# Merging the four score stages of an HGRN2 unit into two runs on TensorE

## The chip, the cores and the metric

The kernel runs on one core of a Trainium2 chip. The metric is the device time of one execution in microseconds (us). Engines are named as in the profile: PE is TensorE (PEld its weight load), DVE is VectorE, ACT is ScalarE, POOL is GpSimd, and SP issues the DMA. Each engine works through its own instructions in the order in which they were built into the program; an instruction that has to wait holds everything behind it on its engine.

## The reference, cut to what matters

One mixer layer on a sequence of 2048 positions and 1024 features. One projection feeds three causal branches; their outputs, each times a SiLU gate, are joined, multiplied by `W_out`, added to the scaled input and normalised.

```python
h = jnp.einsum('bsd,de->bse', x, w_in)
a_u, a_v, a_g, b_val, b_glu, b_g, c_q, c_f, c_i, c_g = jnp.split(h, offsets, axis=-1)
y_a = _sgu_mixer(a_u, a_v, ...) * silu(a_g)          # A: gated 128x128 causal mixing
y_b = _conv_module(b_val, b_glu, ...) * silu(b_g)    # B: GLU, 31-tap causal convolution, LayerNorm
y_c = _hgrn2_mixer(c_q, c_f, c_i, lb, norm_g) * silu(c_g)
y = concat([y_a, y_b, y_c]) @ w_out
return layernorm(ALPHA * x + y)
```

The change is in branch C, a gated linear recurrence with 4 heads of width 128:

```python
f = lb + (1 - lb) * sigmoid(f_logit);  k = 1 - f;  q = silu(q)
# S_t = diag(f_t) S_{t-1} + k_t i_t^T ;  o_t = S_t^T q_t, in chunks:
scores[t, s] = sum_d q[t, d] * k[s, d] * prod(f[s+1 .. t, d])   for s <= t
o = scores @ i + (q * prod f) @ state
```

## The kernel before, in words

**Stages.** The sequence is worked in two halves of 1024 positions, each of two groups of G = 512. A half goes through branch B, branch A (first half here, second half at the end), the values of C (`values`) and then the 8 units of C, one for each head and group: 16 units in all, from about 205 us to 395 us and from about 505 us to 690 us of the span. The last stage is the output product, from about 757 us.

**Projections.** `proj_f` (lines 205 to 213) makes one 128x512 result from 24 matmuls (8 slices of the contraction, each as three products of split high and low parts) in one of 3 PSUM banks with the tag `mm`. A unit of C has three: `pm_f`, `pm_q` and `pm_cg`, 72 matmuls of 512 columns.

**What sets the order.** Around the projections the small steps of the units are woven in by a clock in the program that generates the kernel: after each slice of a projection `tick` moves it on by 0.64, so that a unit lasts 15.36 on it; `later(d, fn)` puts a step on a heap that is due d after now, and `tick` emits what is due (lines 178 to 194). The constants `DST0`, `DST`, `DKT`, `DPST`, `DPO` and `DPT` (line 47) are these delays for branch C. The framework's scheduler then orders each engine's instructions by its own costs; the matmuls marked `pinned` stay in the order in which they were emitted.

**A unit** (`hgrn_unit`, lines 358 to 586). `f` and `K` = 1 - f come from `pm_f` (a sigmoid on ACT, two multiplies on DVE). The silu of `pm_q` goes into the tile `X1`. The scores within a chunk are made by a tree of four stages with blocks of 1, 4, 16 and 64 positions. `stage(0)` and `stage(1)` are each a run of 16 matmuls with 32-column weights (line 406; 80 and 48 columns stream), `stage(2)` 8 with 64-column weights (line 441, 96 columns), `chunk_halves` 4 (line 501, 64 columns). All are fp32, which the profile counts as two instructions a matmul. Behind each run DVE copies the result out of its PSUM bank (tag `sc`, two banks) with `copy_predicated` into `S32` or `ST`, and raises `X`, `T` (products of f) and `K` to the next block size: `K` is multiplied in place, so that the next stage's matmuls read what the last one's DVE work has left. The next stage is due 5.5 later.

Then come `transposes` (`pk`, line 516, of K, in the one bank `tr`; ACT copies it out to `KT`), `states` (`pst`, line 532, in the one bank `st`; DVE makes the new states), `outputs` (`po`, lines 552 and 556, in the one bank `o`; ACT squares and scales it to `os`) and `finish` (`pt`, line 574, again in the one bank `tr`: transposes of `os`; DVE's L576 multiplies `pt` by the gate `sg` and reads the bank for that; then the result goes to DRAM). The bank `tr` is thus taken in turn by `pt` of one unit, `pk` of the next, and by `bb` of branch B's normalisation.

**The last stage's tiles.** `y_steps` loads the branches' outputs (`ry`), makes sums of them (`ysa`, `ysb`) in the pool `stiles`, and splits them into high and low parts; `free_c` closes the pools of C and loads the weights `wob` of the last stage into a new pool `w1`.

Of the kernel before, what the change touches and what calls it, by code (L numbers as in the profile page):

```python
# [11 lines left out]
F32 = mybir.dt.float32  # L12
# [8 lines left out]
P = 128  # L21
# [25 lines left out]
DST0, DST, DKT, DPST, DPO, DPT = 4.5, 5.5, 2.5, 2.0, 2.5, 6.0  # L47
# [37 lines left out]
def _body(tc, nc, d, ctx):  # L85
# [272 lines left out]
    def hgrn_unit(h, g, gi, w, x, pl, vh, ST, S32):  # L358
        nm = f"{h}_{g}"
        wf_, wq, wg = w  # L360
        pf = proj_f(wf_, x, f"f{nm}")
        f = pl.tile([P, G], F32, tag="f", bufs=2, name=f"f{nm}")
        nc.scalar.activation(f, pf, AF.Sigmoid)
        K = pl.tile([P, G], F32, tag="K", bufs=2, name=f"K{nm}")
        nc.vector.tensor_scalar(f, f, oml[:, h : h + 1], lb[:, h : h + 1], ALU.mult, ALU.add)
        nc.vector.tensor_scalar(K, f, -1.0, 1.0, ALU.mult, ALU.add)

        pq = proj_f(wq, x, f"q{nm}")
        X1 = pl.tile([P, P, 11], F32, tag="X1", bufs=1, name=f"X1{nm}")
        nc.scalar.activation(X1[:, :, 7:11], pq.rearrange("p (n j) -> p n j", j=4), AF.Silu)  # L370
        f3 = f.rearrange("p (n j) -> p n j", j=4)
        nc.vector.tensor_mul(X1[:, :, 0:2], X1[:, :, 7:9], f3[:, :, 0:2])
        nc.vector.tensor_mul(X1[:, :, 4:7:2], X1[:, :, 9:11], f3[:, :, 2:4])

        cur = {"X": X1.rearrange("p n (s b) -> p n s b", b=1), "T": f3}

# [15 lines left out]
        def stage(st):  # L392
            b = 4 ** st
            n = G // (4 * b)
            nsc = 10 if st == 0 else 6
            X, T = cur["X"], cur["T"]
            pc = bank("sc", 2, f"sc{nm}_{st}")
            if st < 2:
                npar = 32 // (4 * b)
                w_ = nsc * b * npar  # L400
                pcv = pc[:, : 4 * w_].rearrange("p (c w) -> p c w", c=4)
                for c in range(4):
                    for r in range(4):
                        lo_ = c * P + 32 * r
                        p0 = lo_ // (4 * b)
                        pinned(nc.tensor.matmul(pcv[32 * r : 32 * r + 32, c, :], K[:, lo_ : lo_ + 32],
                                         X[:, p0 : p0 + npar, 1 : 1 + nsc, :],
                                         start=True, stop=True))
# [22 lines left out]
                if st == 1:  # L431
                    for r in range(4):
                        rr = slice(32 * r, 32 * r + 32)
                        nc.scalar.copy(ST[rr, :, rr], S32[rr])
            else:
                w_ = nsc * b
                pcv = pc[:, : 4 * w_].rearrange("p (c w) -> p c w", c=4)
                for c in range(4):
                    for m in range(2):
                        lo_ = c * P + 64 * m  # L440
                        pinned(nc.tensor.matmul(pcv[64 * m : 64 * m + 64, c, :], K[:, lo_ : lo_ + 64],  # L441
                                         X[:, lo_ // 64, 1:7, :], start=True, stop=True))
                for i, (j0, s0, nj) in enumerate(((1, 0, 3), (2, 3, 2), (3, 5, 1))):
                    mo, mw = MOFF[6 + i]
                    for m in range(2):
                        rr = slice(64 * m, 64 * m + 64)
                        nc.vector.copy_predicated(  # L447
                            ST[rr, :, 64 * m + j0 * b : 64 * m + (j0 + nj) * b],
                            msk[rr, mo : mo + mw].unsqueeze(1).to_broadcast([64, 4, mw]),
                            pcv[rr, :, s0 * b : (s0 + nj) * b])  # L450

            if st < 2:
                nb = 4 * b
                Xn = pl.tile([P, n // 4, 7, nb], F32, tag=f"X{nb}", bufs=1, name=f"X{nb}_{nm}")
                Xj = X.rearrange("p (m k) s b -> p m k s b", k=4)
                Tj = T.rearrange("p (m k) j -> p m k j", k=4)
                for k0, sl in ((0, slice(0, 2)), (2, slice(4, 7, 2))):
                    nc.vector.tensor_copy(Xn[:, :, sl, 0:b], Xj[:, :, k0 : k0 + 2, 0, :])
                    nc.vector.tensor_mul(
                        Xn[:, :, sl, b : 4 * b],  # L460
                        Xj[:, :, k0 : k0 + 2, 1:4, :].rearrange("p m k s b -> p m k (s b)"),
                        Tj[:, :, k0 : k0 + 2, 0:1].to_broadcast([P, n // 4, 2, 3 * b]))
# [7 lines left out]
            nc.vector.tensor_mul(T[:, :, 2], T[:, :, 2], T[:, :, 3])  # L470
            nc.vector.tensor_mul(T[:, :, 1], T[:, :, 1], T[:, :, 2])
            Tn = pl.tile([P, n], F32, tag=f"T{4 * b}", bufs=2, name=f"T{4 * b}_{nm}")
            nc.vector.tensor_mul(Tn, T[:, :, 0], T[:, :, 1])
            K4 = K.rearrange("p (n j b) -> p n j b", j=4, b=b)
            if b == 1:
                nc.vector.tensor_mul(K4[:, :, 0:3, 0], K4[:, :, 0:3, 0], T[:, :, 1:4])
            else:
                nc.vector.tensor_mul(K4[:, :, 0:3, :], K4[:, :, 0:3, :],
                                     T[:, :, 1:4].unsqueeze(3).to_broadcast([P, n, 3, b]))
# [572 lines left out]
```

## Time and profile before

| | |
|---|---|
| time, median of 3 runs | 922.21 us (921.29 to 924.45) |
| the profiled execution: its time / its span | 923.13 us / 921.4 us |
| PE busy | 902.0 us, 98% of the span |
| DVE busy | 714.3 us, 78% |
| ACT busy | 392.6 us, 43% |
| granted PE clock, mean | 0.995 |

The span runs from the first to the last instruction; about 1.7 us of the execution lie around it. Busy time of PE counts a matmul from its start to its modelled end, and the ends overlap with the next start. So the start-to-start distances of the timeline tell what a matmul costs on PE, and idle time shows only where PE stood for longer than one matmul's tail.

### The profile page before, as it was taken

Reading aid. Unit: us, or ns where it says so; the run is one execution under the profiler, and the core shown is the slowest. Engines: PE = TensorE matmul, PEld = TensorE weight load, DVE = VectorE, ACT = ScalarE, POOL = GpSimd, SP = SyncE. Lnnn points to the kernel's source line nnn. Section 1 sums busy time; section 2 is a strip of 40 time slices with the busy share of each in tenths; the row PEclk is TensorE's granted clock in tenths of the full one; section 3 lists DMA queues with packets and bytes.
Section 4 is the critical chain, followed back from the end, with each engine's and each line's share of the span. In section 5 each row is a group of like instructions: output and inputs, shape, how many; then the busy total and the mean of one; then the engine's idle time right before and its main releaser. Section 6 shows DMA issues by size and latency. Waiting matters only on the chain.

```text
span 921.4 us, 15037 instructions
## 1 busy us (share of the span) xinstructions
PE 902.0 (98%) x5673; PEld 735.7 (80%) x5673; DVE 714.3 (78%) x1614; ACT 392.6 (43%) x774; POOL 81.9 (9%) x127
## 2 busy tenths in 40 slices
PE   8999999999999999999999999999999999999995
PEld 5889886887777877788888777877899887888885
DVE  6998898946787669997999867778785245898777
ACT  6524355143445336643314444443553343443450
POOL 0001200100010000001000000001012000221122
PEclk9999999999999999999999999999999999999998
DMA  8506797031112103521202111111151598555322
GB/s 267 179 26 222 256 313 235 35 115 36 36 46 70 35 13 127 162 68 58 69 1 92 46 47 47 47 46 47 47 173 58 189 333 277 166 181 181 135 92 91
DMA packets 60808, 107.43 MB, mean 117 GB/s; under 512 B 5312, under 2 KB 21952, under 8 KB 60608
## 3 DMA queue, kind: packets, MB, share of 16 engines
q1 hardware_dynamic: 60736, 106.48, 34.7%
q8 instruction: 44, 0.72, 0.3%
q14 instruction: 28, 0.23, 0.1%
HBM read 75.00 MB, written 31.46 MB: 116 GB/s over the span
## 4 chain that ended last, share of the span: by engine, by line
PE 74%; DVE 12%; DMA 5%; issue 3%; ACT 2%; POOL 2%; SPq 0%; POOLq 0%; DVEq 0%; ACTq 0%
DVE acc L285 5%; PE pm_q L201 3%; PE pm_ci L202 3%; PE pm_ci L203 3%; PE pm_ci L201 3%; PE pm_q L203 3%; PE pm_q L202 3%; PE pm_f L201 3%; PE poz L201 3%; PE pm_cg L201 3%; PE poz L203 3%; PE poz L202 3%; PE pm_f L203 3%; PE pm_cg L202 3%; PE pm_cg L203 3%
## 5 line engine op out<-in xcount | busy, mean ns | idle before, releaser
L285 DVE SCALAR_TENSOR_TENSOR acc<-bh,vec,acc 128x512 f32<-128x512 f32 x240 | 172.0, 748 | 2.7
L148 DVE TENSOR_TENSOR wl<-rw,wh 128x512 fp32r<-128x512 f32 x84 | 56.9, 687 | 19.1 <-ACT wh L147 18.9
L147 ACT CAST wh<-rw 128x512 fp32r<-128x512 f32 x84 | 50.1, 619 | 40.4 <-PE pm_f L202 11.1
L201 PE MATMUL pm_f<-xhix,wh 128*128 128x512 f32 x96 | 41.2, 429 | 0.0
L201 PE MATMUL pm_q<-xhix,wh 128*128 128x512 f32 x96 | 40.6, 423 | 0.0
L561 ACT ACTIVATE jk<-po 128x128 f32<-128x128 f32 x64 | 17.8, 277 | 51.6 <-PE po L556 50.6
L201 PE MATMUL pm_cg<-xhix,wh 128*128 128x512 f32 x96 | 38.9, 406 | 0.0
L203 PE MATMUL pm_f<-xhix,wl 128*128 128x512 f32 x96 | 37.7, 393 | 0.0
L202 PE MATMUL pm_q<-xlox,wh 128*128 128x512 f32 x96 | 37.7, 393 | 0.0
L202 PE MATMUL pm_f<-xlox,wh 128*128 128x512 f32 x96 | 37.6, 392 | 0.0
L203 PE MATMUL pm_q<-xhix,wl 128*128 128x512 f32 x96 | 37.6, 392 | 0.0
L201 PE MATMUL pm_ci<-wh_ci,xhix 128*128 128x512 f32 x96 | 37.6, 391 | 0.0
L203 PE MATMUL pm_cg<-xhix,wl 128*128 128x512 f32 x96 | 37.5, 391 | 0.0
L202 PE MATMUL pm_cg<-xlox,wh 128*128 128x512 f32 x96 | 37.5, 391 | 0.0
L203 PE MATMUL pm_ci<-wh_ci,xlox 128*128 128x512 f32 x96 | 37.4, 390 | 0.0
L202 PE MATMUL pm_ci<-wl_ci,xhix 128*128 128x512 f32 x96 | 37.4, 389 | 0.0
L227 POOL TENSOR_SCALAR crs<-ss 128x4 f32<-128x4 f32 x16 | 3.5, 217 | 362.1 <-ACT jk L561 362.1
L356 ACT COPY vh<-pm_ci 128x512 f32<-128x512 f32 x16 | 9.4, 589 | 56.6 <-PE pm_ci L203 56.6
L447 DVE COPY_PREDICATED ST<-msk,sc 64x192 f32<-64x192 int32 (+2 forms) x96 | 28.7, 299 | 5.3 <-PE sc L441 3.1
L504 ACT COPY ST<-sc 64x128 f32<-64x128 f32 x32 | 8.4, 261 | 50.9 <-PE sc L501 50.7
L566 ACT ACTIVATE os<-po,crs 128x128 f32<-128x128 f32 x64 | 18.3, 369 | 25.0 <-POOL crs L228 25.0
L201 PE MATMUL pm_av<-wh_av,xhix 128*128 128x256 f32 x96 | 28.2, 293 | 0.0
(355 smaller groups left out, 2745.6 us busy)
## 6 DMA issues: line engine op xcount, KB each, us to landing
rw<-wf SPq DMA_DIRECT2D x84, 256.0 KB, 3.2
wob<-wo_dr SPq DMA_DIRECT2D x14, 1024.0 KB, 11.3
xr<-x SPq DMA_DIRECT2D x16, 512.0 KB, 3.9
ry<-y_dr SPq DMA_DIRECT2D x32, 256.0 KB, 2.9
out<-xr SPq DMA_DIRECT2D x15, 512.0 KB, 2.6
wo_dr<-wsh SPq DMA_DIRECT2D x28, 256.0 KB, 3.2
wo_dr<-wsl SPq DMA_DIRECT2D x28, 256.0 KB, 3.0
rx<-xT SPq DMA_DIRECT2D x24, 256.0 KB, 3.4
```

The source lines that it names most:

```text
L147: nc.scalar.copy(hi, src)
L148: nc.vector.tensor_sub(lo, src, hi.bitcast(F32))
L201: nc.tensor.matmul(out, wh, xh, start=first, stop=False, **kw)
L202: nc.tensor.matmul(out, wh, xl, start=False, stop=False, **kw)
L203: nc.tensor.matmul(out, wl, xh, start=False, stop=last, **kw)
L227: nc.gpsimd.tensor_scalar(r, mv_var, scale, EPS, ALU.mult, ALU.add)
L285: nc.vector.scalar_tensor_tensor(a, h[:, k : k + G], vcol(cw + k), a, ALU.mult, ALU.add)
L356: nc.scalar.copy(vh[:, gi * 4 + tt, :], pt)
L447: nc.vector.copy_predicated(ST[rr, :, 64 * m + j0 * b : 64 * m + (j0 + nj) * b], msk[rr, mo : mo + mw].unsqueeze(1).to_broadcast([64, 4, mw]),
L504: nc.scalar.copy(ST[0:64, e:4:2, 64:128], pcv[64 * e : 64 * e + 64])
L561: nc.scalar.activation(jk, po[:, c * P : (c + 1) * P], AF.Square, accum_out=ss[:, c : c + 1])
L566: nc.scalar.mul(os_[:, c * P : (c + 1) * P], po[:, c * P : (c + 1) * P], rs[:, c : c + 1])
```

## The change

The four stages of the scores are cut into two runs. `near` is one run of 32 matmuls (stages of block 1 and 4) into one bank, `far` one of 12 (blocks of 16 and 64) into another. For that, what the second stage of a run needs is made ahead of it:

- a second copy of the keys, `L`, is written from `K` for block 4 as soon as f is there (one multiply of 256 elements and one of 128 a partition on DVE, one copy on ACT), where K was multiplied in place after the first stage by one multiply of 384. `L` is one buffer for all units.
- `raise_x` and `raise_t` are the former ends of the stages. `raise_x(0)` and `prep(1)` now stand ahead of the first run; `raise_x(1)`, `raise_t(1)`, `prep(2)`, `raise_x(2)` and `raise_t(2)` behind it.
- ACT's copies of a run (`side`: K's last quarter from `L`, and four copies of `S32` to `ST`) are emitted 4.5 behind the first run.
- the delays: the first run is due 7.0 after its X (before 4.5), the second 8.0 behind the first, the transposes 5.5 behind the second (2.5), the states 3.0 (2.0), the outputs 3.5 (2.5) and the finish 7.5 (6.0). From X to the finish of a unit it is 34.5 in all, before 34.0.
- `Q64` has two buffers in place of one, and the pool of the last stage's sums (`stiles`) is no longer a pool of its own but `w1`.

The diff, cut to its core (the three `copy_predicated` loops are as before):

```diff
-DST0, DST, DKT, DPST, DPO, DPT = 4.5, 5.5, 2.5, 2.0, 2.5, 6.0
+DNEAR, DFAR, DSIDE, DKT, DPST, DPO, DPT = 7.0, 8.0, 4.5, 5.5, 3.0, 3.5, 7.5
...
+        def raise_x(st):
...
+                for k0, sl in ((0, slice(0, 2)), (2, slice(4, 7, 2))):
+                    nc.vector.tensor_copy(Xn[:, :, sl, 0:b], Xj[:, :, k0 : k0 + 2, 0, :])
+                    nc.vector.tensor_mul(
...
+        def raise_t(st):
...
+            nc.vector.tensor_mul(d2, T[:, :, 2], T[:, :, 3])
+            nc.vector.tensor_mul(d1, T[:, :, 1], d2)
...
+            nc.vector.tensor_mul(Tn, T[:, :, 0], d1)
...
+        cur["T", 0] = f3
+        D = raise_t(0)
+        L = pl.tile([P, G], F32, tag="L", bufs=1, name=f"L{nm}")
+        K0 = K.rearrange("p (n j) -> p n j", j=4)
+        L0 = L.rearrange("p (n j) -> p n j", j=4)
+        nc.scalar.copy(L0[:, :, 3], K0[:, :, 3])
+        nc.vector.tensor_mul(L0[:, :, 0:2], K0[:, :, 0:2], D)
+        nc.vector.tensor_mul(L0[:, :, 2], K0[:, :, 2], f3[:, :, 3])
...
+        def near():
+            pc = bank("sc", 2, f"sc{nm}_0")
+            at = 0
+            for st, Kt, nsc in ((0, K, 10), (1, L, 6)):
...
+                        pinned(nc.tensor.matmul(pcv[32 * r : 32 * r + 32, c, :],
+                                                Kt[:, lo_ : lo_ + 32],
+                                                X[:, p0 : p0 + npar, 1 : 1 + nsc, :],
+                                                start=True, stop=True))
...
+            raise_x(1)
+            raise_t(1)
...
+            nc.vector.tensor_mul(L4[:, :, 0:3, :], L4[:, :, 0:3, :],
+                                 T[:, :, 1:4].unsqueeze(3).to_broadcast([P, 32, 3, 4]))
+            prep(2)
+            raise_x(2)
+            raise_t(2)
...
+            nc.vector.tensor_mul(K16[:, :, 0:3, :], L16[:, :, 0:3, :],
+                                 T[:, :, 1:4].unsqueeze(3).to_broadcast([P, 8, 3, 16]))
...
+            def side():
+                nc.scalar.copy(K16[:, :, 3, :], L16[:, :, 3, :])
+                for r in range(4):
+                    rr = slice(32 * r, 32 * r + 32)
+                    nc.scalar.copy(ST[rr, :, rr], S32[rr])
+
+            later(DSIDE, side)
+            later(DFAR, far)
...
+        def far():
+            b = 16
+            pc = bank("sc", 2, f"sc{nm}_2")
...
+                    pinned(nc.tensor.matmul(pcv[64 * m : 64 * m + 64, c, :], L[:, lo_ : lo_ + 64],
+                                            X[:, lo_ // 64, 1:7, :], start=True, stop=True))
             for c in range(4):
                 e = 64 * (c % 2)
-                pinned(nc.tensor.matmul(pcv[e : e + 64, c // 2, :], K4[:, c, 0, :], Q[:, c, 1, :],
+                pinned(nc.tensor.matmul(pch[e : e + 64, c // 2, :], K4[:, c, 0, :], Q[:, c, 1, :],
                                         start=True, stop=True))
...
         prep(0)
-        later(DST0, lambda: stage(0))
+        raise_x(0)
+        prep(1)
+        later(DNEAR, near)
...
+            stiles.append(w1)
...
-    stiles.append(pool("stiles", stack=es, side="right"))
```

**How it moves PE's instructions.** Two pieces of PE's order at the boundary between two units of the second half, first as it was before. The names are those of the text: `pm_cg` and `pm_f` are projections, `sc` the score runs, `pt` and `pk` the two users of the bank `tr`.

```order
L203 MATMUL pm_cg_3_5636<-xhix_4075,wl_1_5213 128x512
L406 MATMUL sc_3_0_5687<-X_3_5630,K_3_5526 32x80 x16
L201 MATMUL pm_f_2_5752<-xhix_3558,wh_1_5722 128x512
L202 MATMUL pm_f_2_5752<-xlox_3559,wh_1_5722 128x512
L203 MATMUL pm_f_2_5752<-xhix_3558,wl_1_5723 128x512
L574 MATMUL pt_3_5757<-ident,os_3_5621 128x128 x4
```

Behind this `pt` stand 6 matmuls of `pm_f`, the run of line 501, and 12 more, and only then `pk` (line 516); the run of the second stage (48 columns) stands 6 projection matmuls behind that. With the change the piece reads so, from `pt` to the first half of `near`:

```order
L612 MATMUL pt_2_6036<-ident,os_2_5950 128x128 x4
L201 MATMUL pm_f_3_6045<-xhix_4117,wh_1_5756 128x512
L202 MATMUL pm_f_3_6045<-xlox_4118,wh_1_5756 128x512
L203 MATMUL pm_f_3_6045<-xhix_4117,wl_1_5757 128x512
L201 MATMUL pm_f_3_6045<-xhix_4117,wh_1_5756 128x512
L202 MATMUL pm_f_3_6045<-xlox_4118,wh_1_5756 128x512
L554 MATMUL pk_3_6049<-ident,K_3_5609 128x128 x3
L203 MATMUL pm_f_3_6045<-xhix_4117,wl_1_5757 128x512
L201 MATMUL pm_f_3_6045<-xhix_4117,wh_1_5756 128x512
L202 MATMUL pm_f_3_6045<-xlox_4118,wh_1_5756 128x512
L203 MATMUL pm_f_3_6045<-xhix_4117,wl_1_5757 128x512
L459 MATMUL sc_2_0_6062<-X_2_5994,K_2_5897 32x80 x16
```

The row behind it is the run's other half, 16 matmuls of 48 columns. `pk` now follows `pt` after 5 projection matmuls, in 8 of the 16 units exactly so; the run `far` stands 24 projection matmuls ahead of this `pt`.

**How it moves DVE's.** The same unit boundary on DVE before, from the second half of the multiplies on X to L576, which reads `pt` (`T` and `f` are the products of f, `S` is S32).

```order
L478 TENSOR_TENSOR K_2_5270<-K_2_5270,T_1_2_5564 128x8x48
L458 COPY X_1_3_5708<-X_3_5630 128x32x2
L459 TENSOR_TENSOR X_1_3_5708<-X_3_5630,f_3_5524 128x32x2x3
L458 COPY X_1_3_5708<-X_3_5630 128x32x2
L459 TENSOR_TENSOR X_1_3_5708<-X_3_5630,f_3_5524 128x32x2x3
L470 TENSOR_TENSOR f_3_5524<-f_3_5524 128x128
L458 COPY X_1_3_5840<-X_1_3_5708 128x8x2x4 x2
L471 TENSOR_TENSOR f_3_5524<-f_3_5524 128x128
L148 TENSOR_TENSOR wl_1_6269<-rw_1_1_6274,wh_1_6268 128x512
```

From there to L576 there are 8 more rows, four of them copies out of the first stage's bank. With the change the stretch that ends in L614, which now reads `pt`, begins with the two multiplies that write `L` (L434 and L435), the multiplies of K and Q behind `far` (L533 and L534) and the six copies of `far` (L541), and goes on like this:

```order
L440 TENSOR_TENSOR X_2_5994<-X_2_5994,f_2_5895 128x128x2
L441 TENSOR_TENSOR X_2_5994<-X_2_5994,f_2_5895 128x128x2
L390 COPY X_2_2_6000<-X_2_5994 128x32x2 x2
L372 TENSOR_TENSOR X_2_5994<-X_2_5994,f_2_5895 128x128x2
L373 TENSOR_TENSOR X_2_5994<-X_2_5994,f_2_5895 128x128
L391 TENSOR_TENSOR X_2_2_6000<-X_2_5994,f_2_5895 128x32x2x3 x2
L390 COPY X_2_2_6095<-X_2_2_6000 128x8x2x4 x2
L375 TENSOR_TENSOR X_2_2_6000<-X_2_2_6000,T_2_2_5903 128x32x2x4
L377 TENSOR_TENSOR X_2_2_6000<-X_2_2_6000,T_2_2_5903 128x32x4
L413 TENSOR_TENSOR T_2_2_5903<-T_2_2_5903 128x32
L391 TENSOR_TENSOR X_2_2_6095<-X_2_2_6000,T_2_2_5903 128x8x2x12 x2
L614 SCALAR_TENSOR_TENSOR sg_2_5500<-pt_2_6036,vec,sg_2_5500 128x512
```

Nothing of this stretch stands ahead of `far` any more: its first multiply writes the one buffer `L`, which the unit before reads until the eight 96-column matmuls of its `far` are through.

More of the change, by code (lines that the diff above doesn't have):

```diff
@@ new lines, in hgrn_unit @@
+        pf = proj_f(wf_, x, f"f{nm}")
+        f = pl.tile([P, G], F32, tag="f", bufs=2, name=f"f{nm}")
+        nc.scalar.activation(f, pf, AF.Sigmoid)
+        K = pl.tile([P, G], F32, tag="K", bufs=2, name=f"K{nm}")
+        nc.vector.tensor_scalar(f, f, oml[:, h : h + 1], lb[:, h : h + 1], ALU.mult, ALU.add)
+        nc.vector.tensor_scalar(K, f, -1.0, 1.0, ALU.mult, ALU.add)
+        f3 = f.rearrange("p (n j) -> p n j", j=4)
+        cur["T", 0] = f3
+        D = raise_t(0)
+        L = pl.tile([P, G], F32, tag="L", bufs=1, name=f"L{nm}")
@@ L430, in stage @@
                             [:, :, :, s0 * b : (s0 + nj) * b])
[L431 to L450, printed above, removed]
@@ new lines, in near @@
+            later(DSIDE, side)
[3 more added lines that the diff above has]
+            pc = bank("sc", 2, f"sc{nm}_2")
+            pcv = pc[:, : 4 * 96].rearrange("p (c w) -> p c w", c=4)
+            pch = pc[:, 4 * 96 :].rearrange("p (c w) -> p c w", c=2)
+            X, T = cur["X", 2], cur["T", 3]
+            Q = cur["X", 3].rearrange("p (c a) t -> p c a t", a=2)
+            K4 = K.rearrange("p (c a t) -> p c a t", a=2, t=64)
+            for c in range(4):
+                for m in range(2):
+                    lo_ = c * P + 64 * m
+                    pinned(nc.tensor.matmul(pcv[64 * m : 64 * m + 64, c, :], L[:, lo_ : lo_ + 64],
+                                            X[:, lo_ // 64, 1:7, :], start=True, stop=True))
@@ L499, in chunk_halves @@
             for c in range(4):
                 e = 64 * (c % 2)
-                pinned(nc.tensor.matmul(pcv[e : e + 64, c // 2, :], K4[:, c, 0, :], Q[:, c, 1, :],
+                pinned(nc.tensor.matmul(pch[e : e + 64, c // 2, :], K4[:, c, 0, :], Q[:, c, 1, :],
                                         start=True, stop=True))
-            for e in range(2):
-                nc.scalar.copy(ST[0:64, e:4:2, 64:128], pcv[64 * e : 64 * e + 64])
+            nc.vector.tensor_mul(K4[:, :, 0, :], K4[:, :, 0, :], T[:, :, 1:2].to_broadcast([P, 4, 64]))
@@ L505, in chunk_halves @@
             nc.vector.tensor_mul(Q[:, :, 1, :], Q[:, :, 1, :], T[:, :, 0:1].to_broadcast([P, 4, 64]))
-            nc.vector.tensor_mul(K4[:, :, 0, :], K4[:, :, 0, :], T[:, :, 1:2].to_broadcast([P, 4, 64]))
             Tc = pl.tile([P, 4], F32, tag="Tc", bufs=2, name=f"Tc{nm}")
             nc.vector.tensor_mul(Tc, T[:, :, 0], T[:, :, 1])
+            for i, (j0, s0, nj) in enumerate(((1, 0, 3), (2, 3, 2), (3, 5, 1))):
+                mo, mw = MOFF[6 + i]
+                for m in range(2):
+                    rr = slice(64 * m, 64 * m + 64)
+                    nc.vector.copy_predicated(
+                        ST[rr, :, 64 * m + j0 * b : 64 * m + (j0 + nj) * b],
+                        msk[rr, mo : mo + mw].unsqueeze(1).to_broadcast([64, 4, mw]),
+                        pcv[rr, :, s0 * b : (s0 + nj) * b])
@@ L509, in chunk_halves @@
+            for e in range(2):
+                nc.scalar.copy(ST[0:64, e:4:2, 64:128], pch[64 * e : 64 * e + 64])
             cur["Q"], cur["Tc"] = Q, Tc
```

117 lines of the change are left out of this document (51 added, 66 removed).

## The prediction

> **What bounds the kernel now.** I read the page's first part first.
>
> ```profile
> span 921.4 us, 15037 instructions
> PE 902.0 (98%) x5673; PEld 735.7 (80%) x5673; DVE 714.3 (78%) x1614; ACT 392.6 (43%) x774; POOL 81.9 (9%) x127
> ```
>
> PE sets the time: it is idle for 19.4 us of the span. So the change can gain in two ways only: PE's own work gets cheaper, or PE's waits in branch C go. And it can lose in one: a new wait on PE. DVE has 200 us to spare in all, but it matters at each place where PE needs its result at once. The view of PE's waits names those there are today in branch C (us in total, times, longest).
>
> ```profile
> PE pk L516 <- DVE K L506: 2.2, 2, 1.4
> PE bt L317 <- ACT os L566: 1.2, 1, 1.2
> PE pst L532 <- DVE bhn L325: 0.8, 1, 0.8
> PE bb L331 <- DVE sg L576: 0.8, 1, 0.8
> ```
>
> Together 5.0 us. Beside these, PE runs without a gap through all 16 units, and what a score run costs has to be read from the timeline of PE, from start to start. Four places in two units of the first half, one for each kind of run, with the projection matmuls around it:
>
> ```profile
> 303.49 0.39 PE L203 MATMUL pm_cg<-xhi_first,wl 128*128 128x512 f32 x1
> 303.81 0.76 PE L406 MATMUL sc<-X,K 128*32 128x80 f32 x32
> 304.50 0.50 PE L201 MATMUL pm_f<-xhix,wh 128*128 128x512 f32 x1
> 304.83 0.40 PE L202 MATMUL pm_f<-xlox,wh 128*128 128x512 f32 x1
> ...
> 312.08 0.40 PE L203 MATMUL pm_q<-xhix,wl 128*128 128x512 f32 x1
> 312.41 0.55 PE L406 MATMUL sc<-X,K 128*32 128x48 f32 x32
> 312.89 0.50 PE L201 MATMUL pm_q<-xhix,wh 128*128 128x512 f32 x1
> 313.23 0.40 PE L202 MATMUL pm_q<-xlox,wh 128*128 128x512 f32 x1
> ...
> 321.65 0.39 PE L203 MATMUL pm_cg<-xhix,wl 128*128 128x512 f32 x1
> 321.96 0.88 PE L441 MATMUL sc<-X,K 128*64 128x96 f32 x16
> 322.78 0.50 PE L201 MATMUL pm_cg<-xhix,wh 128*128 128x512 f32 x1
> 323.11 0.40 PE L202 MATMUL pm_cg<-xlox,wh 128*128 128x512 f32 x1
> ...
> 328.34 0.39 PE L203 MATMUL pm_f<-xhi_first,wl 128*128 128x512 f32 x1
> 328.57 0.60 PE L574 MATMUL pt<-ident,os 128*128 128x128 f32 x4
> 328.93 0.48 PE L201 MATMUL pm_f<-xhi_first,wh 128*128 128x512 f32 x1
> ...
> 330.17 0.40 PE L203 MATMUL pm_f<-xhi_first,wl 128*128 128x512 f32 x1
> 330.50 0.45 PE L501 MATMUL sc<-Q,K 128*64 128x64 f32 x8
> 330.88 0.50 PE L201 MATMUL pm_f<-xhi_first,wh 128*128 128x512 f32 x1
> 331.21 0.40 PE L202 MATMUL pm_f<-xlo_first,wh 128*128 128x512 f32 x1
> ```
>
> A projection matmul is followed by the next start after 0.23 us (328.34 to 328.57). Around a run it is otherwise: the run starts 0.32 after the last projection matmul, and the second one behind it 0.33 after the first. What a run costs PE is the distance between the two L203 and L202 rows less two ordinary steps of 0.23: 1.34 - 0.46 = **0.88** for the first stage, 1.15 - 0.46 = **0.69** for the second, 1.46 - 0.46 = **1.00** for the third and 1.04 - 0.46 = **0.58** for the fourth. That is 3.15 us a unit, 50 us in 16 units.
>
> **The change part by part.** *Runs joined.* The number of matmuls and their columns are the same; two starts and two ends of runs a unit go. The rows bound the price. At least the two irregular steps go, 0.09 at the entry and 0.10 at the exit: 0.19 for each join, 0.38 a unit, 6.1 us in all. At most everything that does not grow with the columns goes. The first two runs differ by 32 x 32 = 1024 instruction columns and by 0.19 us, which leaves 0.69 - 1.5 x 0.19 = 0.40 us of the second run fixed; the other two differ also by 1024 (16 x 96 less 8 x 64) and by 0.42 us, which leaves 0.58 - 0.21 = 0.37. So 0.77 a unit, 12.4 us in all. Both pairs give nearly the same fixed part, which a start and an end would, so I take the value near the upper end: **-12**.
>
> *The old waits.* The transposes come 5.5 behind the multiply of K, where it was 2.5, so the 2.2 us at `pk` go. The others hang on when branch B's normalisation falls on a bank of branch C, and it does so again at other places; of the 2.8 I take 0.8 as gone. **-3**, with -5 and +2 as ends.
>
> *A new wait at `pk`.* The order put `pk` 5 projection matmuls behind `pt`, and both use the one bank `tr`: `pk` can start only when L614 has read `pt`. Before, L576 had 18 projection matmuls and a run for that. L614 stands at the end of a stretch of DVE's work that can't begin before the eight wide matmuls of `far` are through, since its first multiply writes the one buffer `L`. So two paths run from the start of `far` to `pk`. PE's: 0.82 for the wide part (321.96 to 322.78), 0.21 for the rest by the columns above, 24 projection matmuls of 0.23 and 0.10 for the exit, 0.36 for `pt` (328.57 to 328.93), 5 matmuls and 0.08: 1.03 + 5.62 + 0.36 + 1.23 = **8.24 us**. DVE's begins 0.88 after the start of `far` (the length of that run). Nearly all its instructions stand in one stretch of the trace before, and the rest in single rows of DVE's timeline:
>
> ```profile
> 560.11 0.62 DVE L459 TENSOR_TENSOR X<-X,T 128x192 f32<-128x192 f32 x2
> 560.65 0.42 DVE L505 TENSOR_TENSOR Q<-Q,T 128x256 f32<-128x256 f32 x1
> 560.99 0.42 DVE L506 TENSOR_TENSOR K<-K,T 128x256 f32<-128x256 f32 x1
> ...
> 583.04 0.74 DVE L576 SCALAR_TENSOR_TENSOR sg<-pt,vec,sg 128x512 f32<-128x512 f32 x1
> ...
> 670.43 0.46 DVE L372 TENSOR_TENSOR X<-X,f 128x256 f32<-128x256 f32 x1 [0.16 <-ACT X L370]
> ...
> 672.56 1.55 DVE L447 COPY_PREDICATED ST<-msk,sc 64x192 f32<-64x192 int32 x5
> 674.12 0.56 DVE L478 TENSOR_TENSOR K<-K,T 128x384 f32<-128x384 f32 x1
> 674.59 0.65 DVE L459 TENSOR_TENSOR X<-X,f 128x192 f32<-128x192 f32 x2
> 675.17 0.41 DVE L470 TENSOR_TENSOR f<-f 128x128 f32<-128x128 f32 x1
> ```
>
> From 670.43 to 675.17 DVE does the four multiplies on X, two copies and two multiplies for the next block size, the six copies out of the bank of L441 and one multiply of K: 4.74 us. The new stretch has all that, but for the multiply of K (0.47) four others, three of 256 elements at 0.34 (560.65 to 560.99) and one of 128 at about 0.3: +0.85. It has besides two small copies (0.2), `prep(1)` (two multiplies of 256 and 128, 0.55), a product of f (0.12), the pair of L459 (0.54, from 560.11) and L614 itself (0.74). That is 4.74 + 0.85 + 0.2 + 0.55 + 0.12 + 0.54 + 0.74 = 7.74, and with the 0.88 **8.6 us**. In units that split a weight there, one of 0.6 stands in place of the last three small ones, the same within 0.3. So `pk` waits 0.4 us at least by these rows. More is likely: in the old stretch the copies out of PSUM stand between multiplies that need each other's results, in the new one those stand back to back; seven such places at up to 0.1 make it 1.1. I take 0.7. There are 8 units with exactly 5 matmuls between, and 3 with 7 to 9 that have work of branch B in DVE's stretch and for which I take 1.0: 8 x 0.7 + 3 x 1.0 = **+8.5**. The ends: nothing, if DVE packs as before, and 1.9 a unit for 12 units, 23 us, if in addition a weight split waits there for ACT, at the mean of this row's 19 waits, 1.0 us:
>
> ```profile
> DVE wl L148 <- ACT wh L147: 18.9, 19, 3.0
> ```
>
> *What costs nothing.* DVE gets one multiply more a unit (0.3 us) ahead of `far`, where it waits for PE now; ACT gets two copies more of at most 0.6 each, and is busy 43%. ACT's copy of K's last quarter is due 3.5 ahead of `far`, about 5 us, and holds only ACT's next sigmoid; without that cover `far` would stand for the copy's 0.3 us. `pst` and `po` have more room than before. On SP a unit's store moves with `pt` by 0.5 of the clock. The `ysum` tiles in `w1` put the last loads of the second pair of `ry` behind most of `wob`'s; they are needed some 20 us later, and if not, a product of 12 matmuls, 2.8 us, stands in line behind them.
>
> **The sum.** -12 - 3 + 8.5 = -6.5 us. The profiled execution took 923.13 us (span 921.4 and 1.7 around it), 0.9 above the median of the runs, 922.21. So 916.6 by that execution and **916 us** for the median.
>
> **The rivals.**
>
> *DVE is in time.* `pk` doesn't wait, -15, **907 us**. For it speaks that the margin is only 0.4 us by the rows as they stand; against, that nothing in the stretch can start earlier than `far` ends, and that nothing in it is optional.
>
> *Slower: PE waits for DVE at `pk` in each unit for longer than the joins bring.* Place: the bank `tr` between `pt` and `pk`. With 1.8 us in 12 units it is +21.6 - 15 = +6.6, **929 us**. It decides from a wait of 1.3 us a unit, where 15 us are used up. For it: the split of a weight that stands ahead of L434 in some units, waiting for ACT; against: only every other unit has one.
>
> *A long run doesn't keep the pace of a short one.* `near` is 128 instructions with its weight loads, twice the longest run that the trace shows. If its second half costs what it cost alone, only `far`'s join counts, 16 x 0.37 = 5.9: -5.9 - 3 + 8.5 = -0.4, **922 us**. Against it: matmuls start every 15 ns in the second run now (32 in 0.48 us) with no sign of a limit. [...]
>
> **How the numbers follow.** The forecast has 0.42 (its own range 910 to 921), DVE in time 0.22, the long wait 0.19, the pace 0.17. A measurement of this kernel tells 0.3% from no change, 2.8 us: faster is below 919.4, slower above 925.0. Faster: 0.85 of the forecast, all of the first rival and a little of the last, 0.36 + 0.22 + 0.02 = 0.60. Same: 0.06 + 0.01 + 0.10 = 0.17. Slower: 0.18 + 0.05 = 0.23. The range reaches to the centres of the two outer rivals, 906 to 928, which leaves out about half of each.
>
> **What would show it.** Joins: one run of 64 matmul instructions and one of 24 in PE's timeline, costing about 1.2 us each by the same reading; about 1.6 for the first is the third rival. The wait: a row of PE's waits with `pk` on DVE's L614, 0.4 to 1.1 us each, some 8 to 12 times; its absence is the first rival, a total above 15 us the second. DVE idle at L434 or L435, waiting for `far`. The prediction is wrong if PE's idle time in branch C grows elsewhere, above all at `near` or `far` themselves, or if the last stage, which I have at nothing, moves by more than 2 us.

## The result and the profile after

The changed kernel takes **939.25 us** in the median of five runs (937.98 to 941.97); the kernel before took 923.94 in the same comparison. The ratio is 1.0181, with a 95% interval of 1.0166 to 1.0197: about 16.7 us slower, where 6 us faster was forecast and the range ended at 928.

The profiled execution of the changed kernel took 941.97 us, 2.7 above the median; some 2.4 us of that lie ahead of the first unit (its first `pm_cg` starts at 209.1 us, before at 206.7). That part has nothing to do with the change: in the profiles of this study the same point lies between 204.2 and 211.1. The page's first part, and the view of PE's waits, the rows in branch C (us in total, times, longest):

```profile
span 940.2 us, 15073 instructions
PE 903.6 (96%) x5673; PEld 745.5 (79%) x5673; DVE 723.1 (77%) x1630; ACT 403.2 (43%) x804; POOL 80.3 (9%) x127
```

```profile
PE pk L554 <- DVE sg L614: 20.0, 12, 5.1
PE bb L331 <- DVE sg L614: 2.0, 1, 2.0
PE sc L459 <- DVE X L377: 1.0, 1, 1.0
PE pk L554 <- ACT bsy L334: 0.3, 1, 0.3
```

The wait that the prediction named is there, at its place, on its engine, twelve times; but it is 20.0 us and not 8.5. The joins are there too. PE's timeline around one `near` and one `far`, with the last projection matmul ahead of each run:

```profile
335.88 0.40 PE L203 MATMUL pm_f<-xhi_first,wl 128*128 128x512 f32 x1
336.21 0.76 PE L459 MATMUL sc<-X,K 128*32 128x80 f32 x32
336.79 0.52 PE L459 MATMUL sc<-X,L 128*32 128x48 f32 x32
337.24 0.50 PE L201 MATMUL pm_f<-xhi_first,wh 128*128 128x512 f32 x1
337.58 0.40 PE L202 MATMUL pm_f<-xlo_first,wh 128*128 128x512 f32 x1
...
348.55 0.39 PE L203 MATMUL pm_q<-xhi_first,wl 128*128 128x512 f32 x1
348.87 0.88 PE L527 MATMUL sc<-X,L 128*64 128x96 f32 x16
349.58 0.40 PE L531 MATMUL sc<-Q,K 128*64 128x64 f32 x8
349.91 0.50 PE L201 MATMUL pm_cg<-xhi_first,wh 128*128 128x512 f32 x1
350.24 0.39 PE L202 MATMUL pm_cg<-xlo_first,wh 128*128 128x512 f32 x1
```

By the prediction's own reading `near` costs 1.70 - 0.46 = 1.24 us and `far` 1.69 - 0.46 = 1.23; before, their parts cost 1.57 and 1.58. Each join saves 0.34 us, 10.9 us in 32.

What the prediction doesn't have at all stands behind the longer stalls. PE's timeline around the stall of 2.21 us, and the granted clock in two stretches of equal length around `near` (the columns of a window: busy us and instructions of PE, PEld, DVE, ACT, POOL, then the granted clock, the DMA share and GB/s):

```profile
306.93 0.39 PE L202 MATMUL pm_f<-xlox,wh 128*128 128x512 f32 x1
309.52 0.66 PE L554 MATMUL pk<-ident,K 128*128 128x128 f32 x4 [2.21 <-DVE sg L614]
...
310.71 0.48 PE L203 MATMUL pm_f<-xhix,wl 128*128 128x512 f32 x1
311.12 1.30 PE L459 MATMUL sc<-X,K 128*32 128x80 f32 x32
312.19 0.87 PE L459 MATMUL sc<-X,L 128*32 128x48 f32 x32
312.99 0.80 PE L201 MATMUL pm_f<-xhix,wh 128*128 128x512 f32 x1
313.58 0.63 PE L202 MATMUL pm_f<-xlox,wh 128*128 128x512 f32 x1
314.01 0.53 PE L203 MATMUL pm_f<-xhix,wl 128*128 128x512 f32 x1
314.37 0.39 PE L201 MATMUL pm_f<-xhix,wh 128*128 128x512 f32 x1
```

```profile
311.10:314.30 3.20, 3.20 (x68) 2.87 (x68) 2.48 (x11) 0.90 (x2) 0.00 (x0) 0.50 0.03 8
336.00:339.20 3.20, 3.20 (x74) 2.58 (x73) 2.51 (x9) 0.90 (x2) 0.00 (x0) 1.00 0.07 22
```

From 311.1 to 314.3 PE ran at half clock. From 310.71 to 314.37 are 3.66 us; `near` at 1.24 and four ordinary steps of 0.23 would have taken 2.16. The dip cost **1.5 us**, beside the stall. There are five such dips in the 16 units, each 3.41 us long, behind the stalls of 2.06, 2.21, 2.25, 2.75 and 5.08 us; in the units of the kernel before there was none.

So the difference adds up, measured term by term: joins -10.9; the wait at `pk` +20.0; other waits in branch C -1.7 (5.0 before, 3.3 now); five dips, 5 x 1.5 = +7.5; and 0.15 us for each of ten waits more, +1.5, which the rows of waits leave out (from 306.93 to 309.52 is 2.59, less an ordinary step of 0.23 is 2.36, where the row counts 2.21). Sum +16.4 us, against 16.7 measured. The profiled executions give nearly the same: from the first `pm_cg` to the first product of the last stage (`pod`) it is 576.3 us, before 559.2. This stretch, which leaves out what lies ahead of the units, is called the units' stretch below.

### The profile page after: what moved, and what is told of

It is laid out like the page before. It is cut to its first block, busy times and chain, and to the rows that moved or that the text cites. A ratio compares the mean times of both kernels' runs of the same rounds, so it can differ in the third digit from the quotient of the medians.

```text
span 940.2 us, 15073 instructions
## 1 busy us (share of the span) xinstructions
PE 903.6 (96%) x5673; PEld 745.5 (79%) x5673; DVE 723.1 (77%) x1630; ACT 403.2 (43%) x804; POOL 80.3 (9%) x127
## 4 chain that ended last, share of the span: by engine, by line
PE 63%; DVE 21%; DMA 4%; ACT 4%; issue 4%; POOL 3%; SPq 0%; POOLq 0%; DVEq 0%; ACTq 0%
DVE acc L285 5%; PE poz L201 3%; PE poz L203 3%; PE poz L202 3%; PE pm_ci L202 3%; PE pm_ci L203 3%; PE pm_ci L201 3%; DVE ST L541 3%; PE pm_f L201 3%; PE pm_f L203 2%; PE pm_q L201 2%; PE pm_q L203 2%; PE pm_q L202 2%; PE pm_f L202 2%; PE sc L459 2%
## 5 line engine op out<-in xcount | busy, mean ns | idle before, releaser
L201 PE MATMUL pm_q<-xhix,wh 128*128 128x512 f32 x96 | 38.7, 404 | 0.0
L227 POOL TENSOR_SCALAR crs<-ss 128x4 f32<-128x4 f32 x16 | 6.4, 398 | 362.2 <-ACT jk L599 362.1
L510 ACT COPY ST<-S 32x128 f32<-32x128 f32 x64 | 18.9, 295 | 28.4 <-DVE S L498 27.8
L541 DVE COPY_PREDICATED ST<-msk,sc 64x192 f32<-64x192 int32 (+2 forms) x96 | 28.8, 300 | 2.5
L554 PE MATMUL pk<-ident,K 128*128 128x128 f32 x60 | 10.9, 305 | 20.5 <-DVE sg L614 20.0
L557 ACT COPY KT<-pk 128x512 f32<-128x512 f32 (+1 forms) x16 | 9.0, 561 | 49.9 <-PE pk L554 49.9
```

Source lines behind the costliest of these rows:

```text
L201: nc.tensor.matmul(out, wh, xh, start=first, stop=False, **kw)
L541: nc.vector.copy_predicated(ST[rr, :, 64 * m + j0 * b : 64 * m + (j0 + nj) * b], msk[rr, mo : mo + mw].unsqueeze(1).to_broadcast([64, 4, mw]),
L554: pinned(nc.tensor.transpose(pk[:, c * P : (c + 1) * P], K[:, c * P : (c + 1) * P], ident))
```

## The experiments

**1. `pt` behind `pk`.**

```
-DNEAR, DFAR, DSIDE, DKT, DPST, DPO, DPT = 7.0, 8.0, 4.5, 5.5, 3.0, 3.5, 7.5
+DNEAR, DFAR, DSIDE, DKT, DPST, DPO, DPT = 7.0, 8.0, 4.5, 5.5, 3.0, 3.5, 9.0
```

> The changed kernel with one number different: the transposes of the output (`pt`) come 9.0 of the clock behind `po` where they came 7.5. That puts `pt` behind the next unit's `pk` (6 projection matmuls behind it, where it stood 5 ahead), so `pk` has no longer to wait for L614 to read the bank `tr`; all that is computed is the same. Theory (the loss is the wait at `pk`, 20.3 us in the trace, and the stretches at half clock behind its longest stalls, some 8 us; the joined runs do bring their 11 us): no row of PE's waits at `pk` on L614 above 1 us in total, no dip of the clock in branch C, and a median of 908 to 914 us. Rival (the wait only moves: DVE's stretch is late for whatever comes next, `pt`, `bt`, `pst` or `near`): PE's waits elsewhere in branch C above 10 us and 922 us or more. Second rival (the clock dips because of the long runs of narrow matmuls, not of the stalls): the dips stay, 917 us or more.

917.17 us, ratio 0.9947 (0.9929 to 0.9964). One number takes off 22 us and the kernel is faster than before, though not as fast as the theory had it. The wait at `pk` on L614 is gone; PE's waits in branch C are now these, 7.8 us with one of 0.5 at `pk`:

```profile
PE pt L612 <- ACT KT L557: 2.8, 1, 2.8
PE sc L459 <- DVE X L377: 2.6, 4, 0.9
...
PE bt L317 <- DVE s L578: 1.9, 1, 1.9
```

and two dips of the clock are left. With 10.9 off, 2.8 more in waits and two dips the sum is -5.1, measured -4.9. The profiled execution was the slowest of the twelve (921.51), but what it lost lies ahead of the units (first `pm_cg` at 210.0 us); its units' stretch is 554.5, 4.7 below the kernel before. The theory's 908 to 914 had left these waits out; the first rival fell, the second too (of five dips two are left).

**2. Two buffers for `L`.**

```
-        L = pl.tile([P, G], F32, tag="L", bufs=1, name=f"L{nm}")
+        L = pl.tile([P, G], F32, tag="L", bufs=2, name=f"L{nm}")
```

> The changed kernel with two buffers for `L` in place of one, nothing else. The first multiplies that write `L` (L434, L435, 0.64 us) then needn't wait for `far`. Theory (the stretch of DVE that ends in L614 begins at `far` and is a little too long): these two go ahead of the wait for `far` and the stretch gets 0.6 to 0.7 us shorter where they are in time, so the waits of 0.9 us at `pk` shrink to 0.2 to 0.3 and the sum of PE's waits at `pk` from 20 to 11 to 15 us; some stalls of 2.1 to 2.3 us fall below what makes the clock dip, so 2 to 4 dips are left of 5; 924 to 932 us. Rival (the single buffer of `L` is what makes DVE late altogether): the waits at `pk` go to below 4 us and 908 to 915 us. Second rival (it has no part in it, since the stretch has its other work behind `far` anyway): the waits and the time as they were, 936 us or more.

939.93 us, ratio 1.0203 (1.0183 to 1.0223): nothing gained, the second rival holds, and with it falls a step of the prediction, that the stretch begins at `far` *because* L434 writes the one buffer `L`. DVE's timeline of the kernel with two buffers:

```profile
321.68 0.42 DVE L434 TENSOR_TENSOR L<-K,D 128x256 f32<-128x256 f32 x1
324.87 0.43 DVE L533 TENSOR_TENSOR K<-K,T 128x256 f32<-128x256 f32 x1 [2.78 <-PE sc L531]
```

L434 goes early now, and the queue stops one step further on, at L533, which overwrites what `far`'s last matmuls read. All that stands behind it in the queue, the next unit's multiplies on X among it, starts as late as before.

**3. `near` cut in two**, in the kernel of experiment 1.

```
-        later(DNEAR, near)                      # both stages in one run
+        later(DNEAR - 1.0, near0)               # first stage
...
+            later(0.6, lambda: near(pc))        # second stage, three matmuls on
```

> The kernel with `pt` behind `pk`, but the run `near` again cut in two: the 16 matmul pairs of the first stage three projection matmuls earlier, those of the second where the run stood. DVE's order is the same. Theory (a join saves PE the fixed start and end of a run, 0.34 us by the changed kernel's timeline): 16 x 0.34 = 5.4 us longer than the kernel with the run whole, 3.5 to 7. Rival (a long run doesn't keep the pace of a short one, and joining brings little): within 1.5 us of it. Second rival (the whole gain came from elsewhere, from the waits or the order): no difference either, and no distance of 0.3 us in the starts on PE.

916.82 us against 917.17: no difference in time, against the theory. The starts on PE do show its price (0.89 and 0.68 us where 1.24 stood), 16 x 0.33 = 5.3 us. But the waits are others: 5.7 us in branch C in place of 7.8, and no dip in place of two, 3.0 us. These 5.1 us hide it. That was read afterwards, so it needed a pair of kernels in which nothing else moves: experiment 10.

**4. The spacing alone**, with the four old runs.

```
-DST0, DST, DKT, DPST, DPO, DPT = 4.5, 5.5, 2.5, 2.0, 2.5, 6.0
+DST0, DST, DKT, DPST, DPO, DPT = 4.5, 5.5, 5.5, 3.0, 3.5, 7.5
```

> The kernel before with its four score runs and its copies as they were, and only the later steps spaced as in the change: 5.5, 3.0, 3.5 and 7.5 of the clock for `pk`, `pst`, `po` and `pt` in place of 2.5, 2.0, 2.5 and 6.0. `pt` then stands 5 to 7 projection matmuls ahead of the next `pk` in most units, as in the changed kernel. Theory (the wait at `pk` needs both: `pt` close ahead of `pk`, and the long stretch of DVE behind `far` ahead of the instruction that reads `pt`): DVE's instruction that reads `pt` (L576) has shorter pieces ahead of it, waits at `pk` of 0 to 0.6 us a unit, 0 to 8 us in all, no dips or one; 920 to 930 us. Rival (the spacing alone makes the wait, whatever the runs): PE waits at `pk` for L576 by 15 us or more, and 934 us or more.

929.24 us, ratio 1.0085 (1.0064 to 1.0106). `pt` is as close ahead of `pk` as in the change, and the wait is a fifth of that:

```profile
PE pk L516 <- DVE sg L576: 4.3, 4, 1.7
```

So the distance alone doesn't make it; the rival fell. The kernel loses 7 us in the median, and its profiled execution is 9.5 us longer: 4.1 of these lie in the units' stretch (563.3 us), 3.1 of them waits, 4.4 ahead of the units and 1.0 in the last stage. How much the other executions lose ahead of the units stays open.

**5. Work in the wait.** Matmuls that nobody reads go ahead of `pk` into the free bank `o`.

```
         def transposes():
+            if nm not in NOFILL:
+                du = bank("o", 1, f"du{nm}")
+                for c in range(12):
+                    pinned(nc.tensor.matmul(du[:, c % 4 * P : (c % 4 + 1) * P], ident, ident,
+                                            start=True, stop=True))
```

> The changed kernel with work put into the wait: in the 11 units in which PE waited for L614 at `pk` by 0.8 us or more, 12 matmuls of `ident` with itself (128x128, about 0.11 us each by the rows of `po`, 1.35 us together) go ahead of `pk` into the free bank `o`; nothing reads them. `pk` is then 3 projection matmuls behind `pt`, and DVE decides as before when it can start. First theory (beside the stall itself, each stall of some 2 us costs 1.5 us or so through half a clock granted for 3.4 us behind it): PE's idle at `pk` falls from 20 to about 10 us, the longest but one from 2.8 to below 2, one or two dips are left of five in branch C, and though PE does 15 us more of useless work the time FALLS, by 3 to 4 dips of 1.5 us, to 932 to 936 us. Second theory (the dips in the records cost nothing, only the wait for DVE does): 938.5 to 941 us. If the useless work isn't hidden: above 943 us.

945.65 us: the fill was not hidden. An f32 matmul leaves two records here (the price per matmul had been taken from one), as the view by tile shows, 264 for 132:

```profile
L556 PE MATMUL du<-ident x264: 270/275/422, 256.1 to 700.9; 128*128 128x128 f32 x132
```

and 12 of them took 2.8 us. The experiment failed, since the fill was twice the size meant, but one thing can be read: the two units that had stood for 2.21 and 2.06 us took 25.4 and 25.3 us in place of 26.5 and 26.3, though PE does 2.8 us more in them, while units with the short wait got 1.5 longer. Neither of the two has a dip any more.

**9. Half the fill**, in nine units that branch B doesn't disturb.

```
-                for c in range(12):
+                for c in range(6):
```

> The fill of the wait again, at the size that was meant. In the first try each f32 matmul of `ident` ran as two passes (24 records for 12 matmuls, 2.72 us where 1.35 was meant), so PE did some 30 us of useless work for 20 us of waits, and in two units the free bank was held by branch B. Here: 6 matmuls (1.36 us), and only in the nine units that were free of that and waited by 0.9 us or more. First theory (half a clock for 3.4 us behind a stall of some 2 us costs about 1.5 us): in the three units that stood for 2.1 to 2.25 us the stall is 1.3 to 1.4 and there is no dip behind it, in the short ones the fill is hidden to 0.1 us; 3 x 1.5 = 4.5 us less than the changed kernel's 939.3, so 933 to 936.5 us, with two or three dips left in branch C. Second theory (dips cost nothing): 938.5 to 941 us.

936.99 us (934.29 to 940.84), ratio 1.0152 (1.0126 to 1.0178). In the profiled execution (934.69)

```profile
PE pk L561 <- DVE sg L621: 10.0, 7, 2.7
```

the three stalls are 1.35, 1.20 and 1.13 us, none has a dip behind it, and one dip is left in branch C. The two units that can be compared take 25.4 and 25.3 us again, 1.05 less than without the fill, and the short ones 0.5 more, so the fill isn't quite free. PE does more work in these two units and they end earlier: the dips cost time by themselves, here more than 1 us each. The time of the whole program shows this less clearly, since the stall of 5.08 us is 2.62 here, 2.46 less, more than the fill of 1.36 us accounts for. The median lies 0.5 above the theory's range and below the rival's; the ratio's interval overlaps that of the changed kernel a little, so it is the units of the trace that decide.

**6, 8 and 12. `near` later**, in the kernel of experiment 1: 8.0, 9.0 and 10.0 in place of 7.0.

```
-DNEAR, DFAR, DSIDE, DKT, DPST, DPO, DPT = 7.0, 8.0, 4.5, 5.5, 3.0, 3.5, 9.0
+DNEAR, DFAR, DSIDE, DKT, DPST, DPO, DPT = 9.0, 8.0, 4.5, 5.5, 3.0, 3.5, 9.0
```

> The kernel with `pt` behind `pk`, and the wait ahead of `near` 8.0 of the clock in place of 7.0: `near` and all steps behind it come 6 projection matmuls (1.4 us) later. It takes away what is left of new waits in the trace of the kernel with `pt` behind `pk`: `near` standing for the last multiply of X (four times, 2.6 us in all, with both dips of the clock in branch C behind two of them). Theory (joins worth 10.9 us, and then the waits that are left): these 2.6 and the two dips, some 3 us, go: 910 to 914 us, no dips in branch C. Rival (the lateness only moves again): 916 us or more, with waits of PE at another place of branch C.

> `pt` behind `pk`, and `near` at 9.0 of the clock. Theory: with 8.0 the waits ahead of `near` are gone already, so another 1.4 us of room brings nothing: within 2 us of the kernel with 8.0. If some of the lateness of DVE is longer than 1.4 us (a split of a weight standing for ACT), 2 to 4 us less than with 8.0. If branch C's last unit now ends too late for what follows it, longer by 1 to 3 us.

> `pt` behind `pk`, and `near` at 10.0. With 9.0 the trace has 2.9 us of waits of PE left in branch C. Theory: nothing is left to gain but these, so 906 to 911 us. If the steps of a unit now run into those of the next one (L has one buffer, `near` reads X that the next unit writes): 912 us or more, with new waits.

918.77, **908.74** and 910.12 us; ratios 0.9954 (0.9943 to 0.9966), 0.9860 (0.9840 to 0.9879) and 0.9863 (0.9838 to 0.9887). At 8.0 the theory failed: the waits at `near` and the dips of branch C did go, but 9.4 us of others came, one of 3.3 us at `pst` and four at `pt` for ACT's copy KT among them; the rival that lateness only moves was right there. At 9.0 the profile has no dip but at its very end and of PE's waits in branch C these two:

```profile
PE pt L612 <- ACT KT L557: 1.6, 1, 1.6
PE bt L317 <- ACT os L604: 1.3, 1, 1.3
```

More room than that brings nothing. 908.74 us is the fastest of all kernels tried, 14 us below the kernel before.

**7. `near` cut in two** in the kernel with 8.0, as in experiment 3.

```
-        later(DNEAR, near)
+        later(DNEAR - 0.64, near0)
```

> The same kernel with `near` later, and `near` cut in two again (the first stage's matmuls three projection matmuls ahead of the second's, nothing else moved on PE). The earlier pair of runs came out even, where PE's starts said 5.4 us; theory: there the cut took away a wait for KT of 2.8 us and two dips of the clock, which hid its price, and here these aren't there: 3.5 to 6.5 us longer than the kernel with the run whole. Rival (the join of `near` is worth nothing in time, whatever the starts show): within 1.5 us of it.

922.12 us against 918.77: 3.4 longer, just outside the expected 3.5 to 6.5. Its trace has 6.4 us of waits where the other has 9.4, and two dips more, so again something else moved along, and the medians leave the size open. The units' stretches decide it: 557.6 us against 552.1, 5.4 longer, while the 2.9 us of waits less and the two dips more cancel in them. That is 16 x 0.34.

**10. Both joins undone** in the fastest kernel.

```
-        later(DNEAR, near)
+        later(DNEAR - 0.64, near0)              # first stage; the second 0.6 later
...
-            later(DFAR, far)
+            later(DFAR - 0.64, far)             # third stage
+            later(0.6, lambda: far1(pcv, pch, X, T, Q, K4))   # fourth
```

> The fastest kernel so far (`pt` behind `pk`, `near` at 9.0; 908.7 us) with both joins undone: the first stage's matmuls three projection matmuls ahead of the second's, and the third's three ahead of the fourth's, so that PE has four score runs a unit again; nothing else is moved on PE. In that kernel PE waits for 2.9 us only in branch C, and no dip of the clock is there that could hide or add anything. Theory (0.34 us a join by the starts on PE): 32 x 0.34 = 10.9 us longer, 9 to 12.5; 918 to 921.5 us. Rival (the gain of that kernel comes from the spacing of the steps, not from the joins): 908 to 912 us.

921.56 us, ratio 0.9986 (0.9971 to 1.0002). Against the kernel before, the one is at 0.9860 and the other at 0.9986: 0.0126 x 922.5 = 11.6 us for the joins, and 12.8 by the medians. The waits of PE in branch C are nearly the same (3.7 us where 2.9 stood), no dip is in either, and PE's timeline has four runs in a unit again, of which this is the first:

```profile
332.20 0.40 PE L203 MATMUL pm_f<-xhi_first,wl 128*128 128x512 f32 x1
332.53 0.76 PE L461 MATMUL sc<-X,K 128*32 128x80 f32 x32
333.22 0.50 PE L201 MATMUL pm_f<-xhi_first,wh 128*128 128x512 f32 x1
333.56 0.40 PE L202 MATMUL pm_f<-xlo_first,wh 128*128 128x512 f32 x1
```

The traces agree: the units' stretches differ by 10.9 us (556.7 and 545.8), 0.8 of it waits, and the five units without a wait of PE and without branch B's matmuls take 22.1 to 22.5 us with the joins and 22.8 to 23.2 without, 0.63 to 0.72 more each, which is 10 to 11.5 in 16 units. The theory holds (9 to 12.5 us longer), although 12.8 by the medians is a little above it; the rival falls. The better spacing without joins is worth 0 to 2.7 us against the kernel before by this interval; the joins are nearly the whole gain.

**11. `near` at 9.0 alone**, with `pt` where the change has it.

```
-DNEAR, DFAR, DSIDE, DKT, DPST, DPO, DPT = 7.0, 8.0, 4.5, 5.5, 3.0, 3.5, 7.5
+DNEAR, DFAR, DSIDE, DKT, DPST, DPO, DPT = 9.0, 8.0, 4.5, 5.5, 3.0, 3.5, 7.5
```

> The changed kernel with `near` at 9.0 and `pt` left 7.5 behind `po`: one of the two numbers of the fastest kernel alone. `pt` stands 5 to 9 projection matmuls ahead of `pk` as in the changed kernel. Theory (the place of `pt` makes the wait, and a later `near` doesn't touch it): PE waits at `pk` for L614 by 14 to 25 us, with dips behind the long ones, 933 to 942 us. Rival (what mattered was that DVE was late as a whole, and a later `near` gives it the room): below 5 us at `pk` and below 920 us.

918.31 us, ratio 0.9956 (0.9941 to 0.9971). This theory fell: `pt` stands 5 to 9 matmuls ahead of `pk` as in the change, and yet the wait is a third:

```profile
PE pk L554 <- DVE sg L614: 6.5, 7, 1.9
```

DVE's timeline says why. First a unit of the changed kernel with a wait of 0.93 us, then one of this kernel:

```profile
326.30 0.43 DVE L434 TENSOR_TENSOR L<-K,D 128x256 f32<-128x256 f32 x1 [3.08 <-PE sc L527]
...
327.61 1.96 DVE L541 COPY_PREDICATED ST<-msk,sc 64x192 f32<-64x192 int32 x6
329.60 0.47 DVE L440 TENSOR_TENSOR X<-X,f 128x256 f32<-128x256 f32 x1
...
333.88 0.75 DVE L614 SCALAR_TENSOR_TENSOR sg<-pt,vec,sg 128x512 f32<-128x512 f32 x1
```

```profile
320.00 0.46 DVE L440 TENSOR_TENSOR X<-X,f 128x256 f32<-128x256 f32 x1 [1.26 <-ACT X L439]
...
324.64 0.43 DVE L434 TENSOR_TENSOR L<-K,D 128x256 f32<-128x256 f32 x1 [0.50 <-PE sc L527]
...
330.97 0.75 DVE L614 SCALAR_TENSOR_TENSOR sg<-pt,vec,sg 128x512 f32<-128x512 f32 x1 [0.33 <-PE pt L612]
```

In the changed kernel DVE stands idle for 3.08 us ahead of L434, with the next unit's multiplies on X queued behind it, and L614 behind those, 7.58 us after L434. With `near`, and so `far`, 2.0 of the clock later, the order has the multiplies on X (L440 on) ahead of the wait: they fill the idle time, L614 comes 6.33 us after L434 and now waits for `pt`. The wait at `pk` hangs on what stands between `far` and L614 in DVE's queue, as much as on the place of `pt`.

## Why the prediction was wrong, point by point

*What bounds the kernel*: right. PE sets the time in all the kernels tried, and every gain and loss could be read as PE's own work, PE's waits, or PE's clock. The third is what was missing.

*Runs joined, -12*: right. -10.9 by the starts in the trace, 11.6 to 12.8 by the time and 10 to 11.5 by the units of the traces (experiment 10).

*The old waits, -3*: mis-sized, -1.7. Those at `pk`, `bt` and `pst` went; `bb`'s is 2.0 where it was 0.8, on the same L614, and there is a new one at `near`.

*The new wait at `pk`, +8.5*: **the step that failed.** Place, engine and number of the waits were right, the cause in part (next point), and the size was less than half of what came. In the eight units with 5 matmuls between I took 0.7 each, 5.6 in all; the trace has 0.92 to 0.95 in five of them, close to that (DVE's stretch, summed to 7.74, lasts 8.33 there, from 326.30 to the end of L614 at 334.63), and 2.06, 2.21 and 5.08 in the others, 14.0 in all. In the three with branch B's work I took 3.0 together and it was 5.8. The larger ones have one kind of cause, which I had as the upper end of the range only: something in the stretch waits for ACT. The timelines of ACT and DVE ahead of the wait of 2.06 us:

```profile
583.40 1.14 ACT L604 ACTIVATE os<-po,crs 128x128 f32<-128x128 f32 x4 [1.41 <-POOL crs L228]
584.41 0.64 ACT L147 CAST wh<-rw 128x512 fp32r<-128x512 f32 x1
```

```profile
585.08 0.69 DVE L148 TENSOR_TENSOR wl<-rw,wh 128x512 fp32r<-128x512 f32 x1 [4.02 <-ACT wh L147]
585.69 0.42 DVE L434 TENSOR_TENSOR L<-K,D 128x256 f32<-128x256 f32 x1
```

ACT's scaling of `os` waits for POOL, a cast of a weight is queued behind it, DVE's split behind the cast, and L434 and all the rest behind the split. The prediction has the split ahead of L434 and says that only every other unit has one: it is four of the eleven, and in three of these it waits for ACT by 3.9 to 4.1 us (the stalls of 2.06, 2.25 and 2.75). But the prediction never followed the chain on to ACT and POOL, where `po`, moved as well, put `os` just ahead. The longest wait, 5.08 us, begins in the same way, with 4.2 us of waiting for POOL; behind it DVE's L440 stands for ACT's part of X (L439). In the unit of the 2.21 us it is branch B's product `bsy` that DVE waits for, 1.27 us, also queued on ACT behind `os`.

*The mechanism of that wait*: right in that DVE's stretch behind `far` is too long for PE, wrong in why it begins there. It isn't the one buffer of `L` (experiment 2), but that the next unit's work is queued behind instructions that need `far` (experiment 11). "Nothing in the stretch can start earlier than `far` ends" is how the prediction put it; the multiplies on X could, in another order.

*Left out altogether*: what a stall does to the clock, +7.5 us. With the wait at its measured size and no dip the time would have been some 932; the upper end of the range had no room for it. The units of the kernel before show no dip, and no wait there was longer than 1.4 us. But its trace has one all the same, ahead of the units, where the values of C are made (`pm_ci`), behind two stalls of not quite 1 us close together:

```profile
153.20 0.50 PE L201 MATMUL pm_ci<-wh_ci,xhi_first 128*128 128x512 f32 x1 [0.96 <-ACT wh_ci L147]
154.65 0.79 PE L202 MATMUL pm_ci<-wl_ci,xhi_first 128*128 128x512 f32 x1 [0.95 <-DVE wl_ci L148]
...
157.80 0.40 PE L203 MATMUL pm_ci<-wh_ci,xlo_first 128*128 128x512 f32 x1
```

```profile
150.98:154.38 3.40, 1.54 (x4) 0.48 (x3) 2.52 (x6) 3.37 (x6) 1.17 (x2) 1.00 0.91 293
154.40:157.80 3.40, 3.15 (x7) 2.48 (x8) 3.40 (x7) 2.68 (x4) 0.00 (x0) 0.50 0.79 268
```

From 154.65 to 157.80 seven steps took 3.15 us where 7 x 0.23 = 1.61 is ordinary: the 1.5 us could have been read there. That stalls of 2 us and more were possible was in the range, and their second price should have been.

*What costs nothing*: right for the last stage (from the first `pod` to the end 154.8 us, before 155.5), for DVE's and ACT's few instructions more, and for `ysum`.

*The rivals.* The slower one is what happened: PE waits for DVE at `pk` by more than 1.3 us a unit (20.0 / 12 = 1.7), priced at 929 for a wait near that, the rest being the clock and the old waits; it had 0.19 and deserved most. "DVE is in time" is what experiment 8 makes of the change, at 908.74 for the 907 named. The pace of a long run fell: `near`'s 64 records go from 336.21 to 337.24, 16 ns each, where the two short runs before took 0.69 and 0.48 us for 32 each, 22 and 15 ns.

## What to carry to other kernels

A run of narrow matmuls that interrupts full-width ones cost PE a fixed 0.34 us here, by the starts in the trace, so joining the runs paid; but the engine that works on their results gets all of them at once, and its queue decides whether the gain arrives. Before moving a step, list what stands in that engine's queue between the thing it will wait for and the instruction that someone else waits for, and follow each of these to its own producer, two engines on if need be. Look behind PE's stalls for a second price, in the clock: here 1.5 us by the starts behind the stall of 2.21 us. Half a clock was granted behind five stalls of 2.06 to 5.08 us, and behind two of 0.96 and 0.95 us close together, though not behind every stall of such a length.

## What the runs showed of the hardware that was not expected

The granted clock fell to 0.50 for 3.41 us behind some stalls, and not by their length alone: a stall of 1.90 us had a dip behind it (experiment 1, 0.57 in the mean from 636 to 640 us), stalls of 1.99 (the changed kernel), 2.62 (experiment 9) and 3.27 us (experiment 6) had none. In the kernel before, a dip came behind two stalls of 0.96 and 0.95 us, 1.45 us apart by the starts behind them. What decides between the two cases was not tried: no pair of kernels differs in that alone.

One of POOL's two small instructions ahead of `os` (L227, 128x4) took 3.02 us once in the changed kernel, where its median is 0.19; that is the start of the stall of 5.08 us. Why was not tried. The same instruction of the same unit took 0.19 us in the kernel before.
